# Modulation weights in pairs, head sums with tokens on partitions, first norm's sums moved: one layer of a hybrid diffusion backbone

## The chip, the cores and the metric

One core of a Trainium2 chip runs the whole kernel; the other seven are idle. The core has TensorE (PE in the profile; its weight loads are PEld), VectorE (DVE), ScalarE (ACT), GpSimd (POOL) and SyncE (SP), which issues most loads. The metric is the device time of one execution in microseconds, lower is better. All data is fp32.

## The reference

One layer over 256 latent tokens and 256 context tokens with 1024 channels. What matters here:

```python
mod_l = (silu(c) @ mod_w + mod_b)            # six vectors of 1024: shift, scale, gate, twice
mod_c = silu(c_ctx) @ mod_w + mod_b          # the same for the context tokens
hl = rmsnorm(xl, norm1_g) * (1 + sc1) + sh1  # and hc from the context
a, ga, q, k, v, rx, rg, gcv, gna, grn = split(hl @ in_w + in_b)
# neighbourhood attention, 8 heads of 64: q and k are RMS-normalised per head
p = softmax(concat([qn @ kn_local.T * 64 ** -0.5 + bias, qn @ kn_ctx.T * 64 ** -0.5]))
y = (sigmoid(gcv) * conv + sigmoid(gna) * (p @ v) @ na_out_w + sigmoid(grn) * rnn) @ out_w
xl = xl + g1 * y
xl = xl + g2 * moe(rmsnorm(xl, norm2_g) * (1 + sc2) + sh2)   # 16 experts, two per token
```

The conv branch is a 31-tap depthwise convolution with a layer norm, the recurrent branch two gated linear scans.

## The kernel before

Channels lie on partitions and tokens on the free axis, so that a projection block is 128 output channels by 256 (or, with the context, 512) tokens. To keep fp32 accuracy at the speed of the fast format, every weight and activation is split in a high and a low half, and each step of a product is a triple (`mm3`, L68 to L70): high by high, high by low, low by high. A block has eight triples. Only the third product of a triple, L70, reads the low half of the weight. `split` (L73 and L74) makes the halves: ScalarE the high one, then VectorE the low one.

**Stages.** First norm and modulation (L377 to L509), with a fixed order on PE, ACT and DVE. Then the middle, L515 to about L940: keys, conv inputs, recurrence inputs, values, queries, and three times eight gates, with the branches' own work (convolution taps, recurrence, attention) laid between the blocks. Attention is a generator; `fill` advances the generators by the microseconds that each step claims for PE and DVE in its `yield`. In this stage the order on each engine is made at compile time from the order in which the instructions are written and from when a model believes their inputs to be ready. Then the output projection, the router (L1022 to L1096), and eight pairs of experts (L1352 to L1434) whose weights stream through 35 buffers; pairs with more than 64 tokens take an extra block behind a branch (`further`, L1318).

**The weight stream.** `stream` is one list of 512 KB loads, weights (kind 0) and modulation chunks (kind 1), in the order in which SP issues them. `load_w` puts each in the next of four `raw` buffers (`NRAW`). A weight's buffer is free when its split is done, a modulation chunk's when its products are done. `take_raw` loads ahead until four are in flight; `split_ahead` splits the weight for the next block, into one of two pairs of `w` tiles.

**The later modulation rounds.** `mod_round_b` (L526) computes a modulation vector of 1024: 8 chunks, each 4 products with 32 columns of weights (the conditioning vector `cs`) and 256 moving columns, into four 32-partition strips of one bank, then a copy and two transposes. `rest` runs three such rounds; each block calls `next(rest)` once, behind its own products, and thereby does one chunk. `with_mods(chunks, 1)` puts one chunk behind each weight of the stream.

**Head norms in attention** (L766 to L781). ScalarE squares keys and queries, four channel blocks each; per block a product with `hind` (32 columns, two of them used) sums the squares of the two heads and leaves them with heads on partitions (`hps`). ScalarE copies the sums, PE transposes them (`htp`), and `rsqrt`, eleven small VectorE instructions, makes `hrstd` with tokens on partitions. For each of the four head pairs (L839) the factors are spread to channels and transposed (`psk`, `psq`), multiplied into keys and queries, split, and `scores` makes four scores: three products, bias on VectorE, maximum, exponential on ScalarE with the maximum as bias, sum, scaling. `values` transposes the result and multiplies with the values, two scores later (`DEEP`).

**First norm** (L377 to L389). `sqs` collects the squares of both token sets; `pst` sums them over channels; `rsqrt`, `spread` (`prs`) and a copy give `rstd1`. `m0` is the first quarter's modulation; its products stand half before and half behind `pst`.

## Time and profile before

| | |
|---|---|
| median of three runs | 619.68 us (617.89 to 620.88) |
| the profiled execution | 616.12 us |
| its span, first to last instruction | 614.3 us |
| mean granted TensorE clock | 0.999 |
| PE / DVE / ACT / POOL busy | 580.2 / 349.1 / 259.8 / 19.4 us |
| DMA | 170.65 MB, mean 278 GB/s |

A row of the profile names a line of the code, an engine, an operation and the tiles (out<-in). Matmuls are pipelined: a product of 256 columns is recorded with 0.28 us although the next starts 0.12 us later, so costs are read from starts, not from durations. An fp32 product outside the triples has two records. "Idle" counts only time in which the engine's records leave a hole. L68, L69 and L70 are the three products of a triple whatever the block is; the tile's name tells the block (`gaps`, `aps` conv inputs, `rxps`, `vps`, `qps`, `rgps`, `gps` gates, `bps` branches, `ops` output).

### The profile page before, as it was taken

To read this page: it belongs to the slowest core of one execution; us is meant where nothing else is said; L and a number is where in the kernel's file an instruction comes from. 1 tells how busy PE (TensorE), PEld (TensorE's weight loads), DVE (VectorE), ACT (ScalarE), POOL (GpSimd) and SP (SyncE) were. 2 spreads that over 40 slices of the span, in tenths; PEclk is the share of its full clock that TensorE was granted. 3 is DMA by queue.
4 is the path that set the end of the run, shared out by engine and by line. 5 is a ranking of instruction groups with operands and counts; after the bars stand their busy time and mean duration, and the time that the engine had idled before them with its cause. 6 is when DMAs were issued, how large, how long until landed. Compare 5 with 4: busy or idle time off the path is not lost. (4 is left out here: it accounts for less than half of the span.)

```text
span 614.3 us, 10619 instructions
## 1 busy us (share of the span) xinstructions
PE 580.2 (94%) x4127; PEld 408.1 (66%) x4127; DVE 349.1 (57%) x797; ACT 259.8 (42%) x456; POOL 19.4 (3%) x42
## 2 busy tenths in 40 slices
PE   1899999999999899999999988999999999999986
PEld 0789888778788778888899975335445334454454
DVE  4667899999758968988469554121240314132303
ACT  4345446654598765877545624203012111130101
POOL 0000000000000000103112010000000000000000
PEclk9999999999999999999999999999999999999999
DMA  8983874446853463759969776999999999969961
GB/s 256 367 339 114 310 259 154 137 141 193 278 212 103 138 241 103 236 176 356 313 211 379 283 245 226 388 360 406 402 393 407 407 408 409 398 226 409 409 248 68
DMA packets 51825, 170.65 MB, mean 278 GB/s; under 512 B 5664, under 2 KB 10016, under 8 KB 51744
## 3 DMA queue, kind: packets, MB, share of 16 engines
q1 hardware_dynamic: 46704, 151.26, 67.2%
q0 software_dynamic: 5040, 18.35, 8.6%
q8 instruction: 46, 0.75, 0.5%
q14 instruction: 35, 0.29, 0.1%
HBM read 168.54 MB, written 1.05 MB: 276 GB/s over the span
## 5 line engine op out<-in xcount | busy, mean ns | idle before, releaser
L1162 PE MATMUL ph<-ew,xg 128*64 128x512 f32 (+1 forms) x576 | 115.6, 548 | 3.5 <-PEq L1318 2.8
L73 ACT ACTIVATE w<-raw 128x1024 fp32r<-128x1024 f32 x68 | 71.8, 1056 | 65.6 <-PE gps L69 11.6
L74 DVE TENSOR_TENSOR w<-raw,w 128x1024 fp32r<-128x1024 f32 x68 | 82.9, 1219 | 21.5 <-ACT w L73 20.8
L1162 PEld LDWEIGHTS ph<-ew,xg 128*64 128x64 f32 x576 | 41.5, 137 | 66.0 <-issue 58.3
L70 PE MATMUL gps<-h,w 128*128 128x256 f32 x192 | 55.2, 288 | 1.2 <-DVE w L74 1.2
L68 PE MATMUL gps<-h,w 128*128 128x256 f32 x192 | 56.0, 291 | 0.4 <-DVE y L934 0.4
L69 PE MATMUL gps<-h,w 128*128 128x256 f32 x192 | 54.5, 284 | 0.0
L593 DVE SCALAR_TENSOR_TENSOR cacc<-up,vc,cacc 128x243 f32<-128x243 f32 (+14 forms) x120 | 52.1, 472 | 1.4 <-ACT cacc L585 0.7
L1171 DVE SCALAR_TENSOR_TENSOR he<-sl,gsl,ph 128x256 f32<-128x256 f32 x16 | 7.1, 477 | 77.5 <-PE ph L1162 76.2
L1183 PE MATMUL py<-ew,heT 128*64 128x512 f32 x224 | 49.6, 595 | 1.2 <-ACT heT L1178 0.8
L74 DVE TENSOR_TENSOR ys<-py,ys 128x512 fp32r<-128x512 f32 (+1 forms) x18 | 11.4, 633 | 58.0 <-ACT ys L73 58.0
L68 PEld LDWEIGHTS gps<-h,w 128*128 128x128 f32 x192 | 36.6, 191 | 4.2 <-issue 2.6
L70 PEld LDWEIGHTS gps<-h,w 128*128 128x128 f32 x192 | 36.7, 191 | 2.8 <-issue 1.5
L69 PEld LDWEIGHTS gps<-h,w 128*128 128x128 f32 x192 | 36.7, 191 | 0.9 <-issue 0.7
L1183 PEld LDWEIGHTS py<-ew,heT 128*64 128x64 f32 x224 | 15.5, 137 | 30.8 <-issue 26.0
L1201 DVE SCALAR_TENSOR_TENSOR xl<-scp,g,xl 128x256 f32<-128x256 f32 x72 | 29.2, 475 | 7.5 <-PE scp L1197 7.5
L1167 ACT ACTIVATE sl<-ph 128x512 f32<-128x512 f32 (+1 forms) x9 | 5.0, 550 | 63.1 <-PE ph L1162 40.4
L73 ACT ACTIVATE ys<-py 128x512 fp32r<-128x512 f32 (+1 forms) x18 | 9.9, 550 | 50.5 <-PE py L1183 36.6
L114 POOL DMA_DIRECT2D ew<-in_w_exp x31 | 16.6, 537 | 321.1 <-ACT pp L813 248.8
L1119 ACT ACTIVATE xg<-gps,b2m 128x256 f32<-128x256 f32 x32 | 13.4, 471 | 22.7 <-PE gps L1115 21.8
L349 PE MATMUL mps<-ma,cs 128*32 128x256 f32 (+1 forms) x160 | 10.1, 397 | 13.2 <-DMA ma<-in_mod_a 13.1
L1197 PEld LDWEIGHTS scp<-oT,ys 128*128 128x128 f32 x128 | 15.7, 188 | 6.7 <-issue 5.2
(358 smaller groups left out, 1310.0 us busy)
## 6 DMA issues: line engine op xcount, KB each, us to landing
ew<-in_w_exp SPq DMA_DIRECT2D x161, 512.0 KB, 10.2
raw<-in_w_in SPq DMA_DIRECT2D x40, 512.0 KB, 4.4
ew<-in_w_exp POOLq DMA_DIRECT2D x31, 512.0 KB, 7.3
raw<-in_mod_b SPq DMA_DIRECT2D x28, 512.0 KB, 4.1
ma<-in_mod_a SPq DMA_DIRECT2D x12, 512.0 KB, 10.0
raw<-in_w_br SPq DMA_DIRECT2D x12, 512.0 KB, 4.0
raw<-in_w_out SPq DMA_DIRECT2D x8, 512.0 KB, 7.5
ma<-in_mod_a SPq DMA_DIRECT2D x8, 256.0 KB, 6.7
```

Of the source, the lines that this page charges most:

```text
L68: pe.matmul(ps, wh, xh, start=start, stop=False, skip_group_check=True)
L69: pe.matmul(ps, wh, xl_, start=False, stop=False, skip_group_check=True)
L70: return pe.matmul(ps, wl, xh, start=False, stop=stop, skip_group_check=True)
L73: act.activation(hi, src, AF.Copy)
L74: dve.tensor_tensor(lo, src, r32(hi), op=ALU.subtract)
L114: queue.dma_start(t, w_exp[6 * p + 2 * i + s, :, 1024 * q:1024 * q + 1024])
L593: dve.scalar_tensor_tensor(cacc[:, b, i0:i1], up[:, b, i0 + o:i1 + o], half_d[:, b * 31 + j:b * 31 + j + 1], cacc[:, b, i0:i1], op0=ALU.mu ...
L1119: act.activation(place(k0 + j), ps[:, j, :], AF.Identity, bias=b2m[:, k0 + j:k0 + j + 1])
L1162: pe.matmul(ph[64 * s:64 * s + 64, cols], xg(k)[:, c:c + 64], w[:, at], start=k == 0 and not h, stop=k == KD - 1, skip_group_check=True)
L1183: pe.matmul(py[q][64 * s:64 * s + 64, :], heT[f // 2][:, f % 2, 64 * s:64 * s + 64], ew[p][2][f][s][:, q * 512:q * 512 + 512], start=f == ...
L1197: pe.matmul(ps[:, j, :], rows_(i, m), toks(m), start=(j == 0 and i == 0), stop=i == parts - 1, skip_group_check=True)
L1201: dve.scalar_tensor_tensor(xl[:, m, :], ps[:, j, :], g2[:, m:m + 1], xl[:, m, :], op0=ALU.mult, op1=ALU.add)
```

## The change

1. Modulation chunks come in twos: `with_mods` puts two chunks behind every second weight, `mod_round_b` yields after two chunks, and `rest()` takes a step at every second call.
2. Head sums: the squares become the stationary operand (128 tokens wide) and `hind`, now two columns, the moving one, so that the sums come out with tokens on partitions; six blocks of tokens by four channel blocks are 24 products into one bank. The copies and the six transposes go.
3. The queries are no longer multiplied by their factor: unscaled queries are split and multiplied with the keys, which carry both gains and 1/8 (`kq8`). The bias is divided by the query's factor (`invq`) as it is added, the maximum is multiplied by it, and the exponential applies it as its scale. The transposes `psq` and the products `qn` go.
4. `pst` stands ahead of all of `m0`'s products.

```diff
@@ -129,18 +129,23 @@
 
     mods = [mod_b[s, k, :, 1024 * q:1024 * q + 1024] for s, q in ((0, 0), (0, 1), (1, 0)) for k in range(KD)]
 
-    def with_mods(chunks, n):
+    turn = [0]
+
+    def with_mods(chunks):
+
         o = []
         for x in chunks:
             o.append((0, x))
-            o.extend((1, a) for a in mods[:n])
-            del mods[:n]
+            turn[0] += 1
+            if turn[0] % 2 == 0:
+                o.extend((1, a) for a in mods[:2])
+                del mods[:2]
         return o
 
     stream = [(0, w_k[i]) for i in range(4)]
     stream += with_mods([w_in[4 + i] for i in range(8)] + [w_rx[i] for i in range(4)]
                         + [w_v[i] for i in range(4)] + [w_in[i] for i in range(4)]
-                        + [w_in[12 + i] for i in range(4)], 1)
+                        + [w_in[12 + i] for i in range(4)])
 
     jobs, behind = [], []
     for br in range(3):
@@ -153,7 +158,7 @@
     jobs += behind
     for kind, br, m in jobs:
         if kind == "gate":
-            stream += with_mods([w_in[16 + br * 8 + m]], 1)
+            stream += with_mods([w_in[16 + br * 8 + m]])
         else:
             stream.append((0, w_br[br, m // 2]))
     stream += [(0, w_out[m]) for m in range(8)]
@@ -261,7 +266,7 @@
     dve.tensor_scalar(tri, jp, 0.0, None, op0=ALU.is_gt)
     onesb = pers.tile([128, 128], BF16, name="onesb")
     dve.memset(onesb, 1.0)
-    hind = pers.tile([128, 32], F32, name="hind")
+    hind = pers.tile([128, 2], F32, name="hind")
     dve.memset(hind, 0.0)
     dve.memset(hind[0:64, 0:1], 1.0)
     dve.memset(hind[64:128, 1:2], 1.0)
@@ -277,8 +282,9 @@
     dve.tensor_scalar(half_b, v("in_b", 0, 52), 0.5, None, op0=ALU.mult)
     for x in (half_d, half_r, half_l):
         dve.tensor_scalar(x, x, 0.5, None, op0=ALU.mult)
-    qg8 = pers.tile([128, 1], F32, name="qg8")
-    dve.tensor_scalar(qg8, v("qg"), 0.125, None, op0=ALU.mult)
+
+    kq8 = pers.tile([128, 1], F32, name="kq8")
+    dve.scalar_tensor_tensor(kq8, v("qg"), 0.125, v("kg"), op0=ALU.mult, op1=ALU.mult)
 
     def rsqrt(srcs, n, scale):
 
@@ -375,12 +381,11 @@
     start.enter_context(tc.manual_schedule(engines={mybir.EngineType.PE, mybir.EngineType.Activation,
                                                     mybir.EngineType.DVE}))
     m0 = Mod(0, 0)
-    m0.products(range(2))
     pst = ax_bank((128, 4), "pst")
     for t in range(4):
         pe.matmul(pst[:, t:t + 1], sqs[:, t // 2, (t % 2) * 128:(t % 2) * 128 + 128], ones[:, 0:1],
                   start=t == 0, stop=True, skip_group_check=True)
-    m0.products(range(2, 4))
+    m0.products()
     w0 = split_parts()
     m0.copy()
     w0[0]()
@@ -531,8 +536,10 @@
             for j in range(4):
                 pe.matmul(ps[32 * j:32 * j + 32, :], cs[:, k, :], t[:, 256 * j:256 * j + 256],
                           start=k == 0, stop=k == KD - 1, skip_group_check=True)
-            if k < KD - 1 or out is not set_g2:
+            if (k < KD - 1 and k % 2) if out is not set_g2 else k < KD - 1:
                 yield 0
+        if out is not set_g2:
+            yield 0
         row = work.tile([128, 256], F32, tag="h", name="mrow2", bufs=NSG)
         act.activation(row, ps, AF.Copy)
         if out is set_g2:
@@ -560,14 +567,20 @@
         for f in (set_g1, set_b2m, set_a2m):
             yield from mod_round_b(f, ax_bank)
 
-    rest = mod_rest()
+    rest_steps, turn_ = mod_rest(), [0]
+
+    def rest():
+
+        turn_[0] += 1
+        if turn_[0] % 2 == 0:
+            next(rest_steps, None)
 
     def in_block(name):
         w = take_w()
         ps = mm_bank((128, T), name)
         for k in range(KD):
             proj_block(ps, w, k, slice(k * 128, k * 128 + 128), False, k == 0, k == KD - 1)
-        next(rest, None)
+        rest()
         split_ahead()
         return ps
 
@@ -720,7 +733,7 @@
             proj_block(ps, w, k, slice(k * 128, k * 128 + 128), True, k == 0, k == KD - 1)
         act.activation(rxp[b // 2][:, b % 2], ps.rearrange("p (s t) -> p s t", s=2), AF.Identity,
                        bias=v("in_b", CRX + b))
-        next(rest, None)
+        rest()
         split_ahead()
         if b % 2:
             rec = rnn(b // 2)
@@ -741,7 +754,7 @@
                 pe.matmul(vps[t], H[:, s], wh[:, o:o + 512], start=k == 0, stop=False)
                 pe.matmul(vps[t], H[:, s], wl[:, o:o + 512], start=False, stop=False)
                 pe.matmul(vps[t], L[:, s], wh[:, o:o + 512], start=False, stop=k == KD - 1)
-        next(rest, None)
+        rest()
         split_ahead()
         fill(5.6, 1.2)
     for t in range(4):
@@ -763,22 +776,19 @@
         qkn = [piece(name="qkn") for _ in range(2)]
         hxt = piece(name="hx")
 
-        for n, x in ((4, kb), (2, [qb[:, b, :] for b in range(4)])):
-            hp = ax_bank(name="hps")
+        hp = ax_bank((128, 6, NH), "hps")
+        for o, n, x in ((0, 4, kb), (4, 2, [qb[:, b, :] for b in range(4)])):
             for b in range(4):
                 sq = qkn[b // 2][:, 512 * (b % 2):512 * (b % 2) + 128 * n]
                 act.activation(sq, x[b], AF.Square)
-                pe.matmul(hp[32 * b:32 * b + 32, :128 * n], hind, sq, start=True, stop=True, skip_group_check=True)
-            o = 512 * (n == 2)
-            act.activation(hxt[:, o:o + 128 * n], hp[:, :128 * n], AF.Copy)
-            yield 1.2, 0
-        turned = []
-        for o, n in ((0, 4), (512, 2)):
-            tp = ax_bank((128, n, 128), "htp")
-            for t in range(n):
-                pe.transpose(tp[:, t, :], hxt[:, o + 128 * t:o + 128 * t + 128], ident)
-            turned.append(tp.rearrange("p t (b c) -> p t b c", b=4)[:, :, :, :2])
-        hrstd = rsqrt(turned, 48, 1.0 / HD).rearrange("p (t h) -> p t h", t=6)
+                for t in range(n):
+                    pe.matmul(hp[:, o + t, 2 * b:2 * b + 2], sq[:, 128 * t:128 * t + 128], hind,
+                              start=o == 0 and b == 0 and t == 0, stop=True, skip_group_check=True)
+            yield 0.8 * n, 0
+        hrstd = rsqrt([hp.rearrange("p t h -> p (t h)")], 48, 1.0 / HD).rearrange("p (t h) -> p t h", t=6)
+
+        invq = work.tile([128, 2, NH], F32, name="invq")
+        dve.reciprocal(invq, hrstd[:, 4:, :])
         yield 0, 2.5
         qz = []
         for i in range(2):
@@ -805,12 +815,15 @@
             pe.matmul(ps, qH[:, hh, q], kL, start=False, stop=False)
             pe.matmul(ps, qL[:, hh, q], kH, start=False, stop=True)
             bias = rpb[b][:, hh, 2 - 2 * t:6 - 2 * t, :].rearrange("p a b -> p (a b)")
-            dve.tensor_tensor(ps[:, :T], ps[:, :T], bias, op=ALU.add)
+            h = slice(2 * b + hh, 2 * b + hh + 1)
+            rq = hrstd[:, 4 + t, h]
+            dve.scalar_tensor_tensor(ps[:, :T], bias, invq[:, t, h], ps[:, :T], op0=ALU.mult, op1=ALU.add)
             nm = work.tile([128, 1], F32, tag="nm", name="nm", bufs=4)
             dve.tensor_reduce(nm, ps, axis=AX.X, op=ALU.max, negate=True)
             p = pp[hh][:, t, :]
             rs = work.tile([128, 1], F32, tag="rs", name="rs", bufs=4)
-            act.activation(p, ps, AF.Exp, bias=nm, accum_out=rs)
+            dve.tensor_scalar(nm, nm, rq, None, op0=ALU.mult)
+            act.activation(p, ps, AF.Exp, bias=nm, scale=rq, accum_out=rs)
             ri = work.tile([128, 1], F32, tag="ri", name="ri", bufs=4)
             dve.reciprocal(ri, rs)
             if t:
@@ -837,27 +850,22 @@
                                      op0=ALU.add, op1=ALU.subtract)
 
         for b in range(4):
-            hx = cut(hxt, 0, [6, 2, 64])
-            dve.tensor_copy(hx, hrstd[:, :, 2 * b:2 * b + 2].unsqueeze(3).to_broadcast([128, 6, 2, 64]))
+            hx = cut(hxt, 0, [4, 2, 64])
+            dve.tensor_copy(hx, hrstd[:, :4, 2 * b:2 * b + 2].unsqueeze(3).to_broadcast([128, 4, 2, 64]))
             hx = hx.rearrange("p t h d -> p t (h d)")
             psk = ax_bank(name="psk")
             for t in range(4):
                 pe.transpose(psk[:, t * 128:t * 128 + 128], hx[:, t, :], ident)
-            kn = qkn[b % 2][:, :512]
-            dve.scalar_tensor_tensor(kn, kb[b], v("kg"), psk, op0=ALU.mult, op1=ALU.mult)
+            kn = qkn[b % 2][:, 512 * (b // 2):512 * (b // 2) + 512]
+            dve.scalar_tensor_tensor(kn, kb[b], kq8, psk, op0=ALU.mult, op1=ALU.mult)
             kH, kL = kz[b % 2][:, :512], kz[b % 2][:, 512:]
             split(kH, kL, kn)
-            yield 0.5, 2.3
-            psq = ax_bank((128, T), "psq")
-            for t in range(2):
-                pe.transpose(psq[:, t * 128:t * 128 + 128], hx[:, 4 + t, :], ident)
-            qn = qkn[b % 2][:, 512:512 + T]
-            dve.scalar_tensor_tensor(qn, qb[:, b, :], qg8, psq, op0=ALU.mult, op1=ALU.mult)
+            yield 0.5, 1.9
             qH, qL = qz[b % 2]
             for hh in range(2):
                 s = slice(64 * hh, 64 * hh + 64)
-                split(qH[s, hh, :], qL[s, hh, :], qn[s, :])
-            yield 0.3, 1.2
+                split(qH[s, hh, :], qL[s, hh, :], qb[s, b, :])
+            yield 0, 0.8
             pt = pts[2 * (b % 2):2 * (b % 2) + 2]
             for hh in range(2):
                 for t in range(2):
@@ -915,7 +923,7 @@
             act.activation(sg, psg, AF.Tanh, bias=half_b[:, i:i + 1], scale=0.5)
             held[br, m] = sg
             if (br, m) == (0, 7):
-                for _ in rest:
+                for _ in rest_steps:
                     pass
                 shift_sums()
         else:
```

## Rows read from the trace of the kernel before

**Rows 1.** Page, part 1: busy us, share of the span, instructions of each engine.

```profile
PE 580.2 (94%) x4127; PEld 408.1 (66%) x4127; DVE 349.1 (57%) x797; ACT 259.8 (42%) x456; POOL 19.4 (3%) x42
```

**Rows 2.** Stretches: length; busy (count) of PE, PEld, DVE, ACT, POOL; clock; DMA.

```profile
120.00:140.00 20.00, 20.00 (x100) 14.14 (x99) 19.56 (x39) 9.78 (x11) 0.00 (x0) 1.00 0.42 133
...
240.00:260.00 20.00, 20.00 (x143) 17.43 (x143) 19.35 (x41) 15.94 (x33) 2.39 (x4) 1.00 0.58 185
...
400.00:500.00 100.00, 98.31 (x516) 44.00 (x513) 22.01 (x54) 16.20 (x36) 0.00 (x0) 1.00 1.02 397
```

**Rows 3.** TensorE's waits, whole span: us in total, times, longest.

```profile
PE mps L349 <- DMA ma<-in_mod_a: 13.1, 1, 13.1
...
PE ph L1162 <- PEq L1318: 2.8, 2, 2.6
...
PE gps L70 <- DVE w L74: 1.2, 1, 1.2
```

**Rows 4.** Timeline of PE: start, duration; a lone piece, four chunks in one, last piece.

```profile
25.01 1.93 PE L349 MATMUL mps<-ma,cs 128*32 128x256 f32 x32
...
57.10 0.28 PE L70 MATMUL gaps<-h,w 128*128 128x256 f32 x1
57.31 0.64 PE L532 MATMUL mps<-raw,cs 128*32 128x256 f32 x8
...
58.10 0.28 PE L69 MATMUL aps<-h,w 128*128 128x256 f32 x1
58.22 0.28 PE L70 MATMUL aps<-h,w 128*128 128x256 f32 x1
...
174.99 0.64 PE L532 MATMUL mps<-raw,cs 128*32 128x256 f32 x8
```

**Rows 5.** Timeline of SP, ACT, DVE, PE around one weight of the stream.

```profile
146.84 0.33 SPq L78 DMA_DIRECT2D raw<-in_mod_b  x1
147.26 0.38 SPq L78 DMA_DIRECT2D raw<-in_w_in  x1
...
151.88 1.06 ACT L73 ACTIVATE w<-raw 128x1024 fp32r<-128x1024 f32 x1 [1.36 <-DMA raw<-in_w_in]
...
153.13 1.22 DVE L74 TENSOR_TENSOR w<-raw,w 128x1024 fp32r<-128x1024 f32 x1
...
153.65 0.64 PE L532 MATMUL mps<-raw,cs 128*32 128x256 f32 x8
```

**Rows 6.** Timeline of PE before and after the head sums; the stretch between.

```profile
223.99 0.28 PE L70 MATMUL bps<-bi,w 128*128 128x256 f32 x1
...
224.10:234.20 10.10, 10.10 (x50) 5.01 (x49) 3.74 (x10) 4.93 (x11) 0.00 (x0) 1.00 0.25 97
...
234.31 0.28 PE L70 MATMUL gps<-h,w 128*128 128x256 f32 x1
```

**Rows 7.** Timeline of PE: four records of the layer norm's sums.

```profile
191.41 0.28 PE L69 MATMUL gps<-h,w 128*128 128x256 f32 x1
191.53 0.50 PE L612 MATMUL pv<-ones,sqc 128*128 128x1 f32 x4
...
192.09 0.28 PE L68 MATMUL gps<-h,w 128*128 128x256 f32 x1
```

**Rows 8.** By tile: instructions, shortest/median/longest ns, first and last start, forms.

```profile
L808 DVE TENSOR_TENSOR sps<-sps,rpb x16: 419/424/433, 243.0 to 292.0; 128x256 f32<-128x256 f32 x16
...
L855 DVE SCALAR_TENSOR_TENSOR qkn<-qb,qg,psq x4: 475/475/481, 240.4 to 280.2; 128x256 f32<-128x256 f32 x4
...
L294 DVE TENSOR_SCALAR rq<-pst x1: 163/163/163, 16.4 to 16.4; 128x4 f32<-128x4 f32 x1
```

**Rows 9.** Timeline of DVE and PE around the first norm's sums.

```profile
13.24 0.69 DVE L373 TENSOR_TENSOR nrm<-nrm,sq 128x512 f32<-128x512 f32 x1
...
14.49 1.87 PE L381 MATMUL pst<-ones,nrm 128*128 128x1 f32 x8
16.28 1.08 PE L349 MATMUL mps<-ma,cs 128*32 128x128 f32 x16
```

## The prediction

> **What bounds the kernel now.** I read the page's busy line first: TensorE is busy for 94% of the span and no other engine for more than 57% [rows 1]. A share of busy time is only a hint, so the table by stretches came next: TensorE is full in the middle of the kernel and in the attention stretch, and nearly full among the experts, where the DMA engines are full as well [rows 2]. Which of the two leads there is settled by the list of TensorE's waits: it has 13.1 us before the first products (loads), 2.8 us in two places for the sequencer at the branch of L1318, a longest wait for a split weight of 1.2 us, and no row for an expert's weight anywhere [rows 3]. So from about 20 us to the end the TensorE's queue is the path. A microsecond of TensorE time that is taken out ahead of the experts moves their start, and with it the end, by a microsecond, as long as nothing else becomes late. The expert loads follow buffers that TensorE's own work frees, so they move with it; they are the first thing that would be late next, and that is why the gain is not counted beyond some 7 us.
>
> The clock needs no term: the granted clock is 1.00, the higher level of 2.4 GHz, in every stretch read [rows 2].
>
> **Modulation weights in pairs.** The 24 chunks of the three later modulation rounds are consumed one after each projection block, in 26 pieces between 57.3 and 175.6 us; first and last are [rows 4]. What one piece costs is not its busy time but what it delays. Ordinary products follow each other every 0.12 us (58.10 to 58.22). From the last ordinary product before the piece (57.10) to the second one after it (58.10) it is 1.00 us; without the piece it would be 0.24. A lone piece costs 0.76 us. Its duration is 0.64 us for 8 records, and four chunks in one go last 1.93 us for 32 records [rows 4], so a chunk that is added to a piece costs (1.93 - 0.64) / 3 = 0.43 us. The other 0.33 us is paid once for a piece: the pauses when the engine goes from full-width tiles to 32-column tiles and back. Twelve pieces in place of 26 save 14 x 0.33 = **4.6 us** of TensorE. Products, transposes and bytes stay as they are.
>
> What pairs may cost lies in the loads. All stream chunks share four buffers and go through SP's queue in order. At present a modulation chunk and a weight are sent after each piece: 146.84 and 147.26, at the end of a piece [rows 5]. The weight has landed by 151.88, where ScalarE begins its high half; VectorE ends the low half at 154.35, and the block that wants it starts 0.57 us after the piece at 153.65, thus at 154.22. The third product of each triple needs the low half at 154.46. There is 0.1 us to spare. With pairs, SP sends two modulation chunks and then the weight. The weight's issue keeps its distance from the end of the piece (the first chunk's buffer is free 0.43 us earlier, and the issues are 0.42 apart), but one more transfer of 0.52 MB is ahead of it. At the 397 GB/s that the experts' stretch reaches [rows 2] this is 1.3 us, less the 0.43 us head start: the weight lands 0.9 us later, and the two blocks before its use are shorter by 0.33 us. So the low half would be about 1.1 us late in every pair among the short blocks (four pairs before 86 us, four from 143 us on); the blocks of some 6 us in between have room. Two things cover this. Only the third products need the low half, and first and second products of later steps can be put ahead of them at 0.12 us each, if the order written at compile time does so; and the VectorE queue, which is full at 120 to 140 us [rows 2], has to be on time. The bounds are 0 (all covered) and 8 x 1.1 = 9 us. I take 0.25 us a pair, **2.0 us**, near the covered end, since the longest wait for a low half that the trace has now is 1.2 us, and that one stands behind the convolution, not behind a load [rows 3].
>
> **Head sums.** Now: eight products of 32 columns, each alone as soon as ScalarE has its square, then six transposes. From 223.99 to 234.31 us the stretch takes 10.32 us; of its 50 records two began before 224.1, 16 are sums (two records a product) and 6 transposes, so 26 are ordinary, and with the step at the end 27 x 0.12 = 3.24 us belong to the gates' work [rows 6]. Sums and transposes cost 7.1 us. The four pairs of transposes of the queries' factors (psq) go as well; by the same transposes' spacing (0.11 us a record, as for 128-column weights in [rows 7]) these 8 are 0.9 us. Removed: **8.0 us**. Added: 24 products with 128 columns of weights and 2 moving columns. The nearest rows are the layer norm's sums (1 moving column, same type and weights): 191.41 to 192.09 us with four such records among the gates' products, 0.68 - 0.24 = 0.44, so 0.11 us a record [rows 7]. A product is two records, hence 48 x 0.11 = **5.3 us**; between 0.10 and 0.15 a record this is 4.8 to 7.2. Net **-2.7 us** (-0.8 to -3.2).
>
> **Scores.** Per score VectorE gets one more small instruction (row maximum times the query's factor; the nearest row, 128x4, takes 0.16 us), and the bias becomes a scalar_tensor_tensor (0.475 us by psq's, against 0.424) [rows 8]. 16 x (0.16 + 0.05) = 3.4 us more, with 0.16 for the reciprocal; 4 x 0.475 us for the scaled queries, some 0.5 us of narrower copies and a second source of the square root fall away: about +1 us of VectorE in 60 us. In 224.1 to 234.2 us VectorE is busy 3.74 of 10.1 [rows 6], and in 240 to 260 us 19.35 of 20 [rows 2], so there is little room locally. Who waits is the exponential, then the transposes of its result; the list of TensorE's waits has no row at these transposes [rows 3], as gate products lie between a score and its use. I cost it at 0; without that cover 16 x 0.2 = 3.2 us. ScalarE loses two copies out of the sums, and the scale in the exponential changes no element count: 0.
>
> **First norm.** The sums (1.87 us) go ahead of the first products, which now start when their load ends at 13.1 us [rows 3]. The last square sum ends at 13.24 + 0.69 = 13.93 us, so TensorE starts at 13.95, and the chain from the sums gains 0.5 us [rows 9]. But all products now end at 13.95 + 1.87 + 2 x 1.08 = 18.0 us in place of 17.36, and the modulation's row, its turn and VectorE's use of it come 0.6 us later; the transposes of the norm stand behind that turn in TensorE's queue and can gain little. Take **+0.1 us**, bounds -0.5 to +0.6.
>
> **The sum.** -4.6 + 2.0 - 2.7 + 0 + 0.1 = **-5.2 us**. The profiled execution took 616.12 us, 614.3 of it span, so its like would take 610.9. The median of the three timed runs is 619.68, 3.6 above the profiled one; I put the difference on the median: **614.5 us**.
>
> **The rivals.**
> A, late low halves: 0.6 us a pair in the eight tight pairs eat 4.8 us; -4.6 + 4.8 - 2.7 + 0.1 = -2.4, 617.3 us. For it speaks the 0.1 us of room [rows 5]; against it that third products can be put back.
> B, slower: the same place, with VectorE late on top. Its queue runs without a break where the blocks get short again, and the low half waits there behind convolution work. From 0.9 us a pair (7.2 / 8) the change loses; at 1.6 us it is 12.8 - 7.2 = +5.6, 625.3 us.
> C, the change does not do what it says: the compile-time order puts the chunks of a pair apart again, as some are now (26 pieces for 24 chunks). Then only the head sums are left: 619.68 - 2.6 = 617.1 us.
> D, the branches: TensorE waits 2.8 us for its sequencer at L1318, 2.6 of it in one place [rows 3]. TensorE's stream gets 18 products and 18 weight loads longer ahead of the branches, so another branch may have to wait, or none. One such wait more gives 617.1, one less 611.9 us. The Trainium skill, Runtime: NRT & Kernel Launch, section Instruction fetch mechanics, says that a taken branch whose target is not in the instruction pages on hand stalls until it is fetched; the trace agrees as far as the waits stand at the branch and at no place without one.
>
> **How the numbers follow.** Forecast 0.60 (with the good side of D), A 0.12, C 0.10, bad side of D 0.08, B 0.10. What a measurement of this kernel can tell from no change is about 0.5%, 3.1 us: below 616.6 us is faster, above 622.8 slower. The forecast is faster, A, C and D's bad side are the same, B is slower: 0.60, 0.30, 0.10. The range goes from the forecast with no late half and one branch wait less, 614.5 - 2.0 - 2.6 = 610, drawn in to 610.5 because both together are unlikely, up over A, C and D to 619.5; B and some of the tails stay outside.
>
> **What would show it.** Right: mod products in about 12 pieces of 16 records, 1.07 us each; sums of 0.11 us a record without transposes before the square root; TensorE as full as now from 20 to 365 us, with the router reached 5 us earlier. Wrong: waits of third products for the low half at each second short block (A, B), pieces of 8 records (C), a new wait at L1318's branch (D), or TensorE waiting at the transposes of the exponentials. The prediction is also wrong if experts' weights come late once the experts start earlier.

## The result and the profile after

The changed kernel takes 645.71 us (median of six executions, 636.45 to 648.42), beside 619.08 for the kernel before on the same chip. The ratio is 1.037, with a 95% interval of 1.030 to 1.045; it is taken from the four executions within 1.5% of the fastest, without the two slowest, of which the profiled one is one. The prediction was 614.5 us (610.5 to 619.5), and faster: it has the wrong sign and misses by 31 us.

The profiled execution took 648.42 us, near the upper end of the six. The executions differ chiefly in how long TensorE's clock is at its lower level: the mean granted clock is 0.983 in the one of 636.45 us and 0.965 to 0.968 in those around 646. So sizes below come from one execution, and causes are taken from experiments of their own where there is one.

The page's busy line, as in [rows 1], and the line of part 2 for the granted clock (tenths, 40 slices of the span):

```profile
PE 593.7 (92%) x4145; PEld 429.3 (66%) x4145; DVE 350.1 (54%) x809; ACT 260.2 (40%) x454; POOL 19.7 (3%) x42
...
PEclk9999879999999896799999999999999999989989
```

TensorE is busy 13.5 us longer than before, with work that should be shorter. The dips of the clock line are the first reason: before, the clock rose at 23 us (the products of the keys follow each other every 0.22 us until then and every 0.12 us from then on) and stayed up; here it is at its lower level of 1.2 GHz for 41 us after its first rise. TensorE is busy for 37.7 of these 41 us, work that takes half the time at the higher level, so they cost about 19 us. The stretches show where (columns as in [rows 2], kernel after):

```profile
55.00:91.00 36.00, 31.22 (x241) 28.52 (x240) 27.16 (x62) 14.29 (x21) 0.00 (x0) 0.86 0.68 232
...
236.00:256.00 20.00, 18.52 (x113) 18.22 (x112) 9.00 (x28) 7.52 (x15) 0.00 (x0) 0.66 0.44 155
256.00:276.00 20.00, 13.71 (x73) 11.84 (x73) 13.48 (x32) 10.67 (x21) 0.00 (x0) 0.83 0.17 53
276.00:348.00 72.00, 72.00 (x541) 63.80 (x540) 50.12 (x102) 45.59 (x81) 12.52 (x23) 1.00 0.75 256
```

The second reason is TensorE's waits. The list that answers to [rows 3] (kernel after):

```profile
...
PE ptp L838 <- DVE ri L828: 4.1, 1, 4.1
PE gaps L68 <- ACT w L73: 3.0, 2, 1.6
...
PE gps L1123 <- issue: 2.4, 1, 2.4
PE gps L68 <- DVE y L942: 1.9, 1, 1.9
PE gps L70 <- DVE w L74: 1.8, 2, 1.5
PE gaps L70 <- DVE w L74: 1.8, 2, 1.0
PE bps L68 <- ACT b2r L911: 1.7, 1, 1.7
PE qps L70 <- DVE w L74: 1.7, 2, 1.4
```

Against the kernel before (start of the same instruction in both traces) the delay grows like this: conv inputs +1.5 us, first gate +8.3, first head sum +11.9, first key transposes (`psk`) +16.7, the attention's branch (`bps<-att`) +25.8, router +25.8, end +32.3. The delay grows up to the attention's branch, not at all from there to the router, and by 6.5 us more in the experts, which were not touched.

Three things came as predicted. The later modulation runs in pieces of 16 records (61.65), and a pair costs, between its neighbours at 61.44 and 62.87, 1.43 - 0.24 = 1.19 us, just the 0.76 + 0.43 of the prediction. A head sum's record costs 0.10 to 0.11 us at full clock: the eight from 236.09 to 236.91 take 0.82 us. And the order kept the pairs together, so rival C is out. Timeline of TensorE with one row of ScalarE, kernel after: start, duration, and in brackets the wait and what ended it:

```profile
61.44 0.28 PE L70 MATMUL aps<-h,w 128*128 128x256 f32 x1
61.65 1.07 PE L537 MATMUL mps<-raw,cs 128*32 128x256 f32 x16
...
62.87 0.28 PE L69 MATMUL gaps<-h,w 128*128 128x256 f32 x1
...
69.97 1.06 ACT L73 ACTIVATE w<-raw 128x1024 fp32r<-128x1024 f32 x1 [3.67 <-DMA raw<-in_w_in]
...
71.08 0.39 PE L68 MATMUL gaps<-h,w 128*128 128x256 f32 x1 [1.42 <-ACT w L73]
...
236.09 0.95 PE L785 MATMUL hps<-hind,qkn 128*128 128x2 f32 x8
236.91 0.36 PE L68 MATMUL gps<-h,w 128*128 128x256 f32 x1
...
240.09 0.40 PE L70 MATMUL gps<-h,w 128*128 128x256 f32 x1
```

### The profile page after: what moved, and what is told of

Its sections match the earlier page's. It is cut to its first block, busy times and chain, and to the rows that moved or that the text cites. A ratio compares the mean times of both kernels' runs of the same rounds, so it can differ in the third digit from the quotient of the medians.

```text
span 646.6 us, 10666 instructions
## 1 busy us (share of the span) xinstructions
PE 593.7 (92%) x4145; PEld 429.3 (66%) x4145; DVE 350.1 (54%) x809; ACT 260.2 (40%) x454; POOL 19.7 (3%) x42
## 5 line engine op out<-in xcount | busy, mean ns | idle before, releaser
L1170 PE MATMUL ph<-ew,xg 128*64 128x512 f32 (+1 forms) x576 | 117.6, 555 | 3.5 <-PEq L1326 2.9
L68 PE MATMUL gps<-h,w 128*128 128x256 f32 x192 | 58.7, 306 | 2.7 <-DVE y L942 1.9
L70 PE MATMUL gps<-h,w 128*128 128x256 f32 x192 | 57.2, 299 | 1.8 <-DVE w L74 1.8
L69 PE MATMUL gps<-h,w 128*128 128x256 f32 x192 | 56.9, 296 | 0.0
L606 DVE SCALAR_TENSOR_TENSOR cacc<-up,vc,cacc 128x245 f32<-128x245 f32 (+14 forms) x120 | 51.0, 471 | 1.3 <-ACT cacc L598 0.7
L74 DVE TENSOR_TENSOR ys<-py,ys 128x512 fp32r<-128x512 f32 (+1 forms) x18 | 11.4, 632 | 58.0 <-ACT ys L73 58.0
L68 PEld LDWEIGHTS gps<-h,w 128*128 128x128 f32 x192 | 38.9, 203 | 5.2 <-DVE y L942 2.1
L70 PEld LDWEIGHTS gps<-h,w 128*128 128x128 f32 x192 | 38.7, 202 | 2.5 <-DVE w L74 2.2
L69 PEld LDWEIGHTS gps<-h,w 128*128 128x128 f32 x192 | 39.0, 203 | 0.9 <-issue 0.9
L1191 PEld LDWEIGHTS py<-ew,heT 128*64 128x64 f32 x224 | 15.5, 137 | 30.8 <-issue 26.3
L1123 PE MATMUL gps<-oh,hT 128*128 128x256 f32 x128 | 18.8, 301 | 4.5 <-issue 2.4
L1123 PEld LDWEIGHTS gps<-oh,hT 128*128 128x128 f32 x128 | 17.1, 203 | 8.9 <-issue 7.6
## 6 DMA issues: line engine op xcount, KB each, us to landing
ew<-in_w_exp SPq DMA_DIRECT2D x161, 512.0 KB, 10.2
ma<-in_mod_a SPq DMA_DIRECT2D x12, 512.0 KB, 10.2
```

Source lines behind the costliest of these rows:

```text
L68: pe.matmul(ps, wh, xh, start=start, stop=False, skip_group_check=True)
L69: pe.matmul(ps, wh, xl_, start=False, stop=False, skip_group_check=True)
L70: return pe.matmul(ps, wl, xh, start=False, stop=stop, skip_group_check=True)
L74: dve.tensor_tensor(lo, src, r32(hi), op=ALU.subtract)
L606: dve.scalar_tensor_tensor(cacc[:, b, i0:i1], up[:, b, i0 + o:i1 + o], half_d[:, b * 31 + j:b * 31 + j + 1], cacc[:, b, i0:i1], op0=ALU.mu ...
L1123: pe.matmul(ps[:, j, :], hT[i][t][:, k * 128:k * 128 + 128], oh[t], start=(j == 0 and t == 0 and i == 0), stop=(t == 1 and i == 1), skip_g ...
```

## The experiments

All ratios are to the kernel before on the same chip; its medians were 619.4 to 620.3 us. The three columns of shifts compare one profiled execution with the profiled one of before, which was itself 3.6 us under its median; so the column of the end stands some 3 us too high against the medians. Part of each shift is older than the edits in the middle: the conv inputs start between 0.7 us earlier and 1.6 us later than before's.

| run | edit | median us | ratio (95%) | first gate | attention's branch | end |
|---|---|---|---|---|---|---|
| e1_pairs | pairs alone | 626.81 | 1.011 (1.005 to 1.016) | +4.6 | +8.1 | +13.2 |
| e2_heads | head sums and queries' factor | 631.44 | 1.022 (1.016 to 1.028) | -1.1 | +8.0 | +12.7 |
| e3_first | first norm's sums ahead | 620.29 | 1.001 (0.998 to 1.003) | +0.8 | +0.8 | +4.1 |
| e4_heads_claims | e2, old claims | 625.94 | 1.013 (1.004 to 1.021) | +2.9 | +4.8 | +10.6 |
| e5_sums | head sums alone | 639.07 | 1.029 (1.023 to 1.035) | +1.5 | +15.5 | +27.5 |
| e6_factor | factor alone | 627.02 | 1.011 (1.006 to 1.016) | -0.7 | +5.3 | +8.2 |
| e7_pairs_pe | pairs, loads in the old order | 629.20 | 1.015 (1.010 to 1.021) | +3.8 | +7.2 | +9.9 |
| e8_sums_wide | e5 with 16 columns | 636.74 | 1.026 (1.021 to 1.031) | +0.5 | +12.0 | +23.6 |
| e9_sums_claims | e5, old claims | 633.63 | 1.021 (1.018 to 1.024) | +2.1 | +8.2 | +18.4 |
| e10_claims | before, claims of e5 | 629.42 | 1.016 (1.013 to 1.018) | 0.0 | +8.2 | +12.9 |
| e11_factor_claims | factor, old claims | 625.44 | 1.009 (1.007 to 1.012) | +0.2 | +4.9 | +8.8 |
| e12_pairs_buffers | pairs, six load buffers | 618.01 | 0.997 (0.996 to 0.999) | -3.8 | -1.8 | +0.4 |
| e13_sums_spread | e5, spread among gates | 625.42 | 1.009 (1.006 to 1.012) | -0.1 | -1.9 | +7.2 |
| e14_pairs_buf_shift | e12, shift sums later | 617.69 | 0.997 (0.995 to 0.999) | -3.3 | -2.2 | +1.7 |
| e15_buffers | before, six load buffers | 618.02 | 0.997 (0.994 to 0.999) | -2.8 | -1.3 | +2.6 |
| e16_buf_lag | e15, branches later | 626.91 | 1.012 (1.009 to 1.014) | -1.2 | +8.1 | +11.7 |
| e17_pairs_buf_lag | e12, branches later | 625.88 | 1.009 (1.006 to 1.012) | -3.7 | +6.3 | +11.4 |
| e18_mended | whole change, four mends | 627.08 | 1.012 (1.009 to 1.014) | -3.9 | other order | +10.6 |

### The parts alone

**Pairs alone** (the diff's hunks of `with_mods`, `mod_round_b` and `rest`).

> Only the modulation chunks come in pairs; everything else is as before. Theory (each part costs on its own): the low halves are late in the short blocks and the granted clock falls there, so the first rxps product starts 6 to 8 us later than before (84.98 us) and the whole is 5 to 9 us slower, about 626 us. Rival 1 (pairs are harmless, the head sums carry the whole loss): -4 to -1 us, the rxps start at 82 to 84 us. Rival 2 (pairs disturb the order of all that follows): +20 us or more.

**Head sums and queries' factor alone** (the hunks in `attention`, with `hind` and `kq8`).

> Only the head sums with tokens on partitions and the queries' factor in the exponential; modulation and first norm as before. Theory: the span up to the sums is as before (hps at 224 us), then the granted clock falls to its lower level while the narrow products run and the attention's first scores have no gate products between them; from the first sum to the first product of the output projection it takes 9 to 14 us longer than before (109.65 us), the whole 9 to 15 us slower. Rival 1 (the sums fall only on top of stalls that the pairs made): -3 to 0 us. Rival 2: the same as the whole change, +25 us.

**First norm's sums ahead alone** (the hunk at `pst`).

> Only the first norm's sums stand ahead of the modulation's products. Theory: the granted clock rises a few us later than before (23.0 us), so the conv inputs' first product starts 1 to 2 us later (54.34 us before), the whole is 1 to 2 us slower. Rival (the later end of the modulation alone counts): +0.1 us.

The pairs cost 1.1%, the heads 2.2%, the first norm nothing that can be measured (the rival of e3). The pairs' time is the one expected, its path is not: `rxps` starts 3.3 us later in place of 6 to 8, and the clock does not fall ahead of 220 us. The first two together are some 18 us, and the whole change lost 27. The 9 us beyond their sum have no experiment of their own. The traces show the clock there: ahead of the router it is at the lower level for 3.4 us in e1, 10.2 us in e2 and 34 us in the whole change, and at 72 to 90 us the whole change falls behind waits that e1 has too (1.8 and 0.8, then 1.7 and 1.0 us) without a fall. With the pairs alone the late weights are all there (waits of TensorE, e1_pairs):

```profile
...
PE gaps L68 <- ACT w L73: 3.4, 2, 1.8
...
PE gaps L70 <- DVE w L74: 1.8, 2, 1.0
PE qps L70 <- DVE w L74: 1.7, 2, 1.4
```

### The planner's claims

**Head sums and factor with the claims of before.**

```diff
-            yield 0.8 * n, 0
+            yield 1.2, 0
-            yield 0.5, 1.9
+            yield 0.5, 2.3
-            yield 0, 0.8
+            yield 0.3, 1.2
```

> As the heads alone, but the steps claim the times that they claimed before the change (1.2 us each for the two sums' steps, 2.3 and 1.2 us of VectorE for the two preparations). Theory that the claims let the attention run ahead of the gates: the wait of the exponentials' transposes (4.1 us in the whole change) is gone and it is 4 to 8 us faster than the heads alone. Rival (the narrow products themselves cost the clock, whatever lies around): within 2 us of the heads alone.

**Head sums alone, with the changed kernel's claim.** The products `qn` and the scores stay as before.

> The head sums alone in the changed form (48 products of 2 columns, old claims of the queries' part, the queries' factor still multiplied in ahead of the scores). Theory 1, narrow products and the wait for the split weight behind them pull the granted clock down: TensorE waits 1.5 us for the gate's weight low half behind the sums, the clock is at its lower level for one to three stretches of 3.4 us between the sums and the scores, and the 2.7 us that the sums save are lost: 620 to 623 us. Theory 2, the sums do what the prediction's term says and the queries' factor alone costs: 617.5 us and no stretch at the lower level.

**The kernel before with that claim and nothing else.**

```diff
             act.activation(hxt[:, o:o + 128 * n], hp[:, :128 * n], AF.Copy)
-            yield 1.2, 0
+            yield 0.8 * n, 0
```

> The kernel before with the two PE claims of the head sums raised from 1.2 and 1.2 to 3.2 and 1.6, and no other edit. Theory 1, the larger claim by itself makes the planner draw more attention steps behind one gate, so that TensorE waits 3 to 4 us for the first transpose of the exponentials and the clock falls there, and not among the head sums: 623 to 630 us. Theory 2, the claims alone do nothing (before's longer sums cover them): 619 to 621 us.

**Head sums alone, with the claims of before.**

```diff
-            yield 0.8 * n, 0
+            yield 1.2, 0
```

> The head sums alone in the changed form, but with the PE claims of the kernel before (1.2 twice, where the changed form claims 3.2 and 1.6). Theory 1, two separate causes, narrow products for the clock and the larger claims for the packed scores: the 3.6 us wait for the first transpose of the exponentials is gone, the clock still falls among the head sums at 228 to 231 us with no wait ahead of it, and the time is 624 to 632 us. Theory 2, the clock falls only because the claims pack the steps together: no fall before 300 us and 617 to 619 us, the saving that the prediction gave.

The claim of 3.2 and 1.6 us for the head sums' TensorE time is closer to the 5 us that their 48 records take (at 0.10 to 0.11) than the old one of 1.2 twice, and by itself it costs 1.6%. `fill` draws attention steps until the VectorE microseconds asked for exceed the TensorE microseconds by one; a larger claim for TensorE makes it draw more steps at once. The scores then stand one behind the other with no gate's products between a score and its transposes, and TensorE waits for the exponentials. Timeline of TensorE in the kernel before with that claim (e10_claims), and the two stretches around it:

```profile
248.32 1.08 PE L825 MATMUL ptp<-ident,pp 128*128 128x128 f32 x4 [3.87 <-DVE ri L815]
...
253.60 0.39 PE L68 MATMUL gps<-h,w 128*128 128x256 f32 x1 [1.40 <-DVE y L934]
```

```profile
239.00:247.90 8.90, 4.88 (x31) 3.90 (x29) 8.36 (x16) 4.13 (x10) 0.00 (x0) 1.00 0.38 122
248.00:251.40 3.40, 3.08 (x12) 2.71 (x13) 1.54 (x6) 1.80 (x4) 0.00 (x0) 0.50 0.00 0
```

The clock falls at that wait: 3.4 us at half speed, with TensorE busy for 3.1 of them, add 1.5 us. With the old claims the wait is gone in both kernels (e4 and e9), and their medians are 5.5 and 5.4 us below their partners' (e2 and e5), with intervals that touch. That is the theory of e4 and theory 1 of e10; theory 1 of e9 had wait and fall right, and its time is 1.6 us above the range. The head sums alone came out slower, at 639.07 us, than either theory of e5 had it, since wait and falling clock add up there: 24 us at the lower level ahead of the router, 17 us from the router's counts on. So the 4.1 us wait of the changed kernel is a matter of the claims, and not of the added VectorE work of a score: this measured 16 x 0.206 us for the maximum and 16 x 0.06 for the bias, and it is in e4 as well.

### The clock among the narrow products

**Head sums alone with 16 moving columns, 14 of them zero.**

```diff
-    hind = pers.tile([128, 2], F32, name="hind")
+    hind = pers.tile([128, 16], F32, name="hind")
-        hp = ax_bank((128, 6, NH), "hps")
+        hp = ax_bank((128, 24, 16), "hps")
```

> As the run with the head sums alone, with 16 columns to each of the 48 products (14 of them zero) instead of 2. Theory 1, the clock falls because the narrow products leave TensorE little to do: fewer stretches at the lower level than with 2 columns, and up to 3 us less time for all that each product is no shorter. Theory 2, it falls for the wait behind the sums: the same wait, the same stretches, and the same time within 0.3%.

**Head sums alone, a gate's products between their groups** (the `yield` moves into the loop over `b`).

```diff
-            yield 0.8 * n, 0
+                yield 0.3, 1.2
```

> The head sums alone in the changed form, with a gate's 24 products between groups of 8 or 16 narrow records (each group yields to the planner, claims 0.3 and 1.2). Theory 1, narrow products close together make the clock fall: no fall from the first head sum to the first scores, and the first key transposes no later against the gates' products than in the kernel before; 617 to 624 us, the order behind it differing too. Theory 2, the clock falls for the form of the products wherever they stand: at least one stretch at the lower level among them, and 628 us or more.

In the run with the sums alone and the old claims the clock falls at 229.3 us, when the sums are 3 us old. TensorE has had no wait over 0.4 us since 214.1, and it is busy without a hole. From there to 246.4 us all its records are at half speed. The same 48 records, spread over 17 us with gates and branches between them, leave the clock where it is. Stretches of e9_sums_claims and then of e13_sums_spread:

```profile
226.00:229.30 3.30, 3.30 (x32) 3.30 (x31) 2.24 (x8) 2.31 (x6) 0.00 (x0) 1.00 0.83 297
229.40:239.00 9.60, 9.60 (x46) 9.60 (x46) 0.40 (x2) 2.77 (x4) 0.00 (x0) 0.50 0.01 3
239.00:246.30 7.30, 6.25 (x29) 5.96 (x29) 4.57 (x13) 0.52 (x2) 0.00 (x0) 0.50 0.43 144
```

```profile
223.00:247.00 24.00, 23.96 (x204) 23.72 (x202) 13.76 (x32) 10.73 (x17) 0.06 (x1) 1.00 0.45 165
```

What differs in this stretch is how close together the narrow products stand: e9 has 48 of them with 24 ordinary ones between, e13 with 96. All six kernels with the sums close together (the changed one, e2, e4, e5, e8, e9) lost the clock among them or at the wait right behind; the runs with the old sums, and the two with spread ones (e13, e18), did not. Sixteen columns in place of two do not keep the clock up: it falls at 228.2 us in e8. The numbers are still those of its theory 1, 31 us at the lower level over the whole kernel in place of 41 and a median 2.3 us lower; but the intervals overlap, and the order is another (e8 begins with 16 narrow records in a row), so e8 settles nothing. Theory 1 of e13 held for the clock, not for the time. That the clock falls where narrow products are packed is shown; why it does stays open. The Trainium skill, TensorE: Matmul & The Clock Gate, section A second HAM failure mode: psum-queue depth-cycling, tells of a kernel whose clock goes to and fro because TensorE idles very briefly, and often, between groups of products. Here the trace shows no idle time at all at the fall; no run here shows whether idle parts hidden inside the narrow records count.

The spread sums also fit the term's sign and rough size: the attention's branch starts 1.9 us earlier than before's (0.1 us of it are there at the first gate), against the 2.7 of the prediction. They still lose 9 us, behind that branch (below).

### The queries' factor

**Factor alone, with the changed claims.**

> The queries' factor in the exponential alone, with the changed claims (0.5, 1.9 and 0, 0.8), the head sums as before. Theory 1, the claims no longer pull gate products in between the scores and the transposes of the exponentials, so TensorE waits 4 us for the first of them and 1.6 to 1.9 us for the gate behind them, with a stretch at the lower clock after each: 624 to 629 us. Theory 2, that wait belongs to the head sums' place and not to the factor: 619 to 621 us.

**Factor alone, with the claims of before.**

```diff
-            yield 0.5, 1.9
+            yield 0.5, 2.3
-            yield 0, 0.8
+            yield 0.3, 1.2
```

> The queries' factor in the exponential alone, with the claims of the kernel before (0.5, 2.3 and 0.3, 1.2). Theory 1, what the factor cost in its own run (+6.9 us) comes from its smaller VectorE claims, which leave fewer gate products between the steps: the waits of 1.5 us at the first scores and behind them go, and the time is 617 to 620 us. Theory 2, the three added small VectorE instructions and the longer chain from the scores to the exponential cost it: 623 to 627 us.

The factor alone costs what theory 1 of e6 said, but its waits are others: none at the exponentials' transposes, 1.5 us at the first scores and 1.5 us at the gate behind them. Theory 1 of e11 fell: the claims are worth 1.6 us of median at most; the wait at the gate goes with them, those at `psk` and at the first scores stay. The time is that of theory 2, but the trace names a cause that no theory had. The unscaled queries need no factor, so their splits are ready early, and the order made at compile time puts four of them (0.41 us each) and one more split of a weight (1.2 us) among the small steps of the square root on VectorE. From the first of these steps to the copy of the factors (`hx`) it takes 9.4 us, before 7.0; the reciprocal `invq` is only 0.25 us of that. The same four splits stand in the changed kernel, e2, e4 and e6. Timeline of VectorE, kernel before and then e11_factor_claims:

```profile
238.08 0.56 DVE L841 COPY hx<-rq 128x768 f32<-128x768 f32 x1
```

```profile
236.45 0.41 DVE L74 TENSOR_TENSOR qz<-qb,qz 64x256 fp32r<-64x256 f32 x1
...
240.59 0.25 DVE L783 RECIPROCAL invq<-rq 128x16 f32<-128x16 f32 x1
240.76 0.36 DVE L846 COPY hx<-rq 128x512 f32<-128x512 f32 x1
```

So the first `psk` comes behind a finished branch; the `psq` transposes and the gate's and branch's products that lay between `psk` and the first scores are gone from that place, and the scores wait for the keys' split. No run put the queries' splits back behind the square root. Timeline of TensorE and a stretch, e11_factor_claims:

```profile
241.27 0.63 PE L850 MATMUL psk<-ident,hx 128*128 128x128 f32 x4 [1.11 <-DVE hx L846]
243.40 1.17 PE L806 MATMUL sps<-kz,qz 128*128 128x512 f32 x3 [1.50 <-ACT kz L73]
```

```profile
244.00:247.40 3.40, 3.40 (x11) 2.54 (x10) 2.39 (x6) 1.25 (x3) 0.00 (x0) 0.50 0.53 154
```

Waits of 2.6 us where the kernel before has 0.5, and 3.4 us at half speed behind them (1.7 us), are 3.8 of the 4.9 us that this part has lost at the attention's branch. A second cost is on ScalarE: with a scale read for each partition the exponential takes 0.777 us in place of 0.687. By tile, kernel after and then kernel before (shortest, median, longest ns):

```profile
L826 ACT ACTIVATE pp<-sps,nm,rq x16: 765/777/779, 262.5 to 311.8; 128x512 f32<-128x512 f32 x16
```

```profile
L813 ACT ACTIVATE pp<-sps,nm x16: 680/687/699, 244.4 to 293.2; 128x512 f32<-128x512 f32 x16
```

### The pairs and the load buffers

**Pairs on TensorE, loads in the order weight, chunk, weight, chunk.**

> Modulation pieces worked off two chunks at a time as in the changed kernel, but the loads in the old order (weight, modulation chunk, weight, modulation chunk). Theory 1, the late weights of the pairs come from two modulation chunks standing between two weights in the load queue: the waits of 1.0 to 1.8 us for a weight at 70 to 84 us go, and the time is 616 to 619 us, the 14 pieces' gain showing. Theory 2, they come from the four load buffers, of which two now come free at one time whatever the order: the waits stay and the time is 624 to 628 us.

**Pairs with six load buffers.**

```diff
-NPC, NRAW, NW, NSG, NSQ = 35, 4, 2, 6, 2
+NPC, NRAW, NW, NSG, NSQ = 33, 6, 2, 6, 2
```

> The pairs alone with six load buffers instead of four (two fewer of the 35 buffers that pieces and experts share). Theory 1, the weights are late in the pairs because two of the four load buffers stay with modulation chunks until both are worked off: the waits of 1.0 to 1.8 us at 70 to 84 and 155 us go, the head sums start 2 us earlier than before's instead of 8 us later, and the time is 614 to 619 us unless the smaller ring of the experts costs it. Theory 2, the weights are late for their splits on ScalarE and VectorE and not for the loads: the waits stay, and the head sums start 6 to 8 us later than before's.

**The same two buffers for the kernel before.**

> The kernel before with six load buffers instead of four (33 shared ones instead of 35), and no other edit. Theory 1, the buffers mend only what the pairs break: the time is that of the kernel before within 0.4%. Theory 2, the buffers themselves bring the gain of the run with pairs and six buffers: 617 to 618.5 us.

The order of the loads does not mend it (theory 2 of e7, though 629.20 us is above its range): in the old order the waits only move (2.4 us at a modulation piece, 1.9 and 1.0 at the queries), and the pairs come apart, in 18 pieces in place of 12. The buffers are the cause (theory 1 of e12). Two of four hold modulation chunks until the pair is worked off, then both come free at once, and the next weight's load starts too late; in e1 the loads of two chunks are sent together at 60.01 us, and those of two weights at 61.69. With six, every weight wait over 0.5 us ahead of 200 us is gone, and the gates start 3.8 us earlier than before's. (The head sums do not start 2 us earlier, as e12 expected, but 1.4 us later.) But the kernel before with six buffers is as fast, 618.02 beside 618.01 us (theory 2 of e15; the range of its theory 1 holds this time too). The saving itself is there: counted as in the prediction, the 12 pieces of e12 cost 16.1 us, the 24 of e15 20.3 (1.19 and 0.76 us each, more beside products of the values and the recurrence). Waits of 1.5 us that e15 lacks take part of it, so that at the first gate the pairs are 1.0 us ahead of the buffers alone (1.8 counted from the conv inputs), and at the end nothing is left. The next three runs ask where it goes.

**Six buffers, pairs, and the shift sums (`b2r`) issued behind the second branch.**

```diff
-                for _ in rest_steps:
-                    pass
-                shift_sums()
+                for _ in rest_steps:
+                    pass
...
+            if (br, m) == (0, 2):
+                shift_sums()
```

> The pairs with six load buffers, and the shift sums issued two branch jobs later than in the kernel before. Theory 1, TensorE's 3.4 us wait behind the first gates and the 10 us at the lower clock around it came from the shift sums' wait for ScalarE: both go, bps<-att starts 5 to 7 us earlier than before's and the time is 612 to 615 us. Theory 2, the convolution's halves, which the same branch reads, are late as well (VectorE and ScalarE set the pace there): a wait of 2 us or more stays in the same place under another name, and the time is 616 to 619 us.

**Six buffers and the branches one pair of gates later, without and with pairs.**

```diff
-NPC, NRAW, NW, NSG, NSQ = 35, 4, 2, 6, 2
+NPC, NRAW, NW, NSG, NSQ = 33, 6, 2, 8, 2
-LAG, DEEP = 3, 2
+LAG, DEEP = 4, 2
```

> The kernel before with six load buffers and the branches one pair of gates later (LAG 4, eight gate buffers). Theory 1, the first branch's input set the pace ahead of 210 us: the 3.4 us wait there and the stretch at the lower clock around it go, and the time is 611 to 615 us. Theory 2, the attention's own chain or the experts take it back: 617 to 619 us.

> The same with the modulation in pairs. Theory 1, the pieces' gain was taken by the wait for the first branch's input and shows when that is gone: 1 to 4.6 us less than the run without the pairs. Theory 2, the pairs gain nothing or lose even with buffers and without that wait: within 0.3% of the run without the pairs.

In e14 the edit moved almost nothing: the order made at compile time still puts the copy of the sums (`b2r`, at 209.18 us; 208.69 in e12) straight ahead of the first branch, and only the product behind it comes later (210.48 in place of 209.35). So e14 does not test its theories; that its time lies in the range of theory 2 is no more than e12 repeated. What tests the sums is e16 and e17, where a gate comes first: the wait does not care what stands first behind it. It is 3.4 us ahead of the first branch (e12, e14, e15), and when a gate is put there instead, it is 3.8 us ahead of the gate. First rows of TensorE's waits from 60 to 215 us, of e12_pairs_buffers, then e15_buffers, then e17_pairs_buf_lag:

```profile
PE bps L68 <- ACT b2r L916: 3.4, 1, 3.4
```

```profile
PE bps L68 <- ACT b2r L903: 3.4, 1, 3.4
```

```profile
PE gps L68 <- ACT w L73: 3.8, 1, 3.8
```

It always ends at 208.8 to 211.8 us, and always at ScalarE. The stretch ahead of it, in the kernel before, e15_buffers and e17_pairs_buf_lag (columns as in [rows 2]; the fourth busy time is ScalarE's):

```profile
170.00:209.00 39.00, 37.85 (x294) 33.43 (x293) 29.93 (x65) 35.59 (x57) 0.00 (x0) 1.00 0.45 148
```

```profile
170.00:209.00 39.00, 36.16 (x276) 31.87 (x274) 32.18 (x68) 36.06 (x55) 0.00 (x0) 1.00 0.39 136
```

```profile
170.00:209.00 39.00, 35.16 (x272) 30.71 (x270) 33.43 (x70) 36.81 (x56) 0.00 (x0) 1.00 0.39 135
```

ScalarE is busy 35.6 of 39 us even in the kernel before; in its rows the splits of weights stand behind the copies of the convolution and the recurrence's functions, with table loads of 1.28 us between (three from 202.0 to 207.4 us in e15). So in these runs what TensorE saved ahead of 209 us was waited out there, and the clock falls at that wait in e12 and e14 to e17 (6.8 or 10.2 us at the lower level). Both theories of e16 fell, with 626.91 us: up to the attention's branch the later branches lose 9.4 us against e15, of which 4 us are new waits (1.3, 0.9 and 1.4 us of them in the attention); the rest was not traced. e17 is left undecided: it is 1.0 us faster than e16, with intervals that overlap, at the edge of theory 1 and within the 0.3% of theory 2. Nothing was tried that takes work off ScalarE, so that it sets the pace there is read from the traces and not shown by an experiment.

### The whole change, mended

Six buffers, LAG 4, head sums spread with claims 0.3 and 2.0, the factor's claims as before.

> The whole change (pairs, head sums, queries' factor, first norm's sums ahead) with four mends: six load buffers, branches one pair of gates later, the head sums in groups of 8 narrow records with at least a gate's products between most of them (claims 0.3 and 2.0), and the factor's claims as before. Theory 1, what the change lost is the late weights, the clustered narrow products and the packed scores: no stretch at the lower clock and no wait over 1.5 us between 60 and 245 us, and 610 to 618 us. Theory 2, the queries' factor or the later attention still costs: a wait or a fall between the first key transposes and the attention's branch, and 619 to 626 us.

Its median is 18.6 us below the changed kernel's, it has the clock up from 215 to 331 us, and it still loses 1.2%: theory 2 by its sign, 1.1 us above the range and not in the place it named. The 3.8 us wait for ScalarE at 209 us and its fall are there, 2.4 us of waits for weights in the attention's branch with a fall, and 8 us in the experts.

## Why the prediction was wrong

**"The clock needs no term"** is the step that failed most. It read the clock as a property of the kernel before [rows 2], and not as something the change could lose. Of the 32 us between the two profiled executions about 19 are the cost of time at the lower level: 34 us ahead of the router and 6.8 us in the experts, with TensorE busy for 37.7 of these.

**The pairs, -4.6 + 2.0.** The price of a piece was right (1.19 us). Two terms around it were not. The late weights were taken near the covered end; they measured 3.4 + 1.8 + 1.7 us, and 1.4 us at `rgps`, 8.3 us in all in e1, near the upper bound of 9. Not only third products wait, as the step had it, but first ones too, for the high half: the whole weight is late. The step reckoned with one more transfer ahead of the weight, and overlooked that two buffers now come free together. Rival A had the mechanism, rival B the sign and, by chance, nearly the size (625.3 us; the pairs alone gave 626.81), but put the blame on VectorE's queue; six load buffers remove the waits, so it was not VectorE. And the rule that a microsecond ahead of the experts moves the end by a microsecond "as long as nothing else becomes late" was checked in three stretches [rows 2], not in 170 to 209 us, where ScalarE was already busy for 35.6 of 39 us. The saving of -4.6 shows with six buffers: from the conv inputs to the first gate e12 takes 117.8 us, the kernel before 122.6. But the buffers alone already give 3.1 of these 4.8 us (e15, where no piece is split in two and no wait is left), and what the stretch has gained by the first gate is lost in 170 to 209 us.

**Head sums, -2.7.** The record's price held at 0.11 us, and spread out they gave -1.9 us at the attention's branch. Packed, as the change has them, they cost the clock: 5.2 us between first head sum and first key transposes when alone (e9). The nearest row [rows 7] was right for the price and blind for this: four such records stood there alone among the gates.

**Scores, "I cost it at 0; without that cover 16 x 0.2 = 3.2 us".** The cover went, by the claims and not by the instructions, and the price was not 16 x 0.2: one wait of 4.1 us, one of 1.9, and a fall at each, 9 us from `psk` to the attention's branch. The step counted the scaled queries that fall away as a saving for VectorE, and did not ask what the unscaled ones would do in its queue: their splits come in among the steps of the square root, and alone (e11) the first `psk` starts 2.5 us later. "[T]he scale in the exponential changes no element count: 0" missed 16 x 0.09 = 1.4 us on ScalarE, which the trace of before could not show.

**First norm, +0.1.** Right within the measurement: 620.29 beside 620.32 us. The clock's first rise comes at 27.3 us there and 28.5 in the changed kernel, against 23.0 before, but at 28 us in e14 and e16 too, which lack this edit.

**Experts and rival D.** In the changed kernel no wait of the experts is for a load. (In e1, e2, e10 and e18 the wait of 2.6 to 2.8 us that the others have for the branch of L1318 bears the name of one.) But TensorE waits for "issue", for nothing that the profile shows, ahead of the experts' gathers (`gps<-oh,hT`) in all eight kernels with the new head sums: 2.4 us in the changed one, 1.8 to 2.2 in the others that have the factor too, 4.3 to 4.8 in the four without it. In the twelve other kernels it is 0.5 us at most. The four have such a wait at the experts' first products as well, in all 7.2 to 7.9 us, which is most of what they lose behind the router (9 to 12 us). Of them e13 (waits of TensorE from 330 us on):

```profile
PE gps L1109 <- issue: 4.3, 1, 4.3
PE ph L1156 <- issue: 3.6, 2, 1.8
```

The kernel before has 0.8 us of it in the same stretch, all at the first products, and the other eleven up to 1.9. The prediction's list of the waits for the branch of L1318 was short by one row of the kernel before:

```profile
PE gps L1115 <- PEq L1318: 1.4, 2, 0.9
```

Rival D foresaw this (2.6 us more or less when TensorE's stream changes its length), at the branch; it came at products. By the Trainium skill, Runtime: NRT & Kernel Launch, section Instruction fetch mechanics, a branch to code that is not on hand stalls. That fits a wait that depends on how many instructions stand ahead; that it is the fetch is argued, not shown, and stays open.

## What to carry to other kernels

Ask first which engine would be late next in each stretch that the saved time has to pass, and read the busy table there: here a stretch with another engine at 91% took a gain away. Work that an edit frees from a dependency may run earlier than before, in the way of something else; look where it goes in the other engines' queues. Here products with few moving columns were as cheap as their spacing said only while they stood among wide ones; keep them spread. And where a planner works with claimed times, a claim is part of the kernel: changing one to a truer value cost 1.6% here without any other edit.

## What the runs showed of the hardware

The clock fell to 1.2 GHz with TensorE recorded busy throughout, in 48 packed records of 2 or 16 columns. It also falls at short waits, but not always: all kernels here wait the same 2.8 us ahead of the router's counts (`pk`; 369.16 us in the kernel before, 394.94 after), and the clock falls there in 13 of the 18 kernels of the study, and in neither the profiled execution of before nor that of after. From that wait to the experts' first product the kernels without a fall agree within 0.02 us; a fall cost 0.5 to 1.1 us there (in e18 a wait of 1.1 us comes on top). So two kernels with equal work can differ by several falls, which is the size of the effects sought here. Row of the kernel before:

```profile
369.16 0.18 PE L1084 MATMUL pk<-maskb,tri 128*128 128x16 bf16 x1 [2.83 <-DVE maskb L1061]
```

The only gain found is the plain one: six load buffers in place of four, with no other edit, give 618.02 us, 0.997 (0.994 to 0.999) of the kernel before; the pairs on top of them add nothing.
